# Softmax minus one-hot over 8192 rows: loads row by row, the sixth row in two column halves

## The chip, the cores and the metric

The kernel runs on one NeuronCore of a Trainium2 chip. The metric is the device time of one execution in microseconds (us). The runs before the change took 1247.62, 1247.97 and 1248.04 us, median 1247.97 us. A profiled execution beside them gives the trace that is read here; its span, from the first to the last recorded instruction of the core, is 1245.7 us.

The engines that matter are VectorE (DVE), ScalarE (ACT), SyncE (SP), which issues the loads, and the 16 DMA engines of the core, which carry out loads and stores alike. ScalarE issues the stores beside its computing. Each issuing engine has a DMA queue of its own: the profile calls SyncE's q1 and ScalarE's q10.

## The reference

The inputs are logits of 8 x 1024 x 8192 in float32 and one label for each of the 8192 positions. For each row of 8192 values the result is the softmax minus a one at the label:

```python
logits_max = np.max(logits, axis=-1, keepdims=True)
exp_logits = np.exp(logits - logits_max)
softmax = exp_logits / np.sum(exp_logits, axis=-1, keepdims=True)
...
one_hot[batch_idx, seq_idx, labels] = 1.0
return (softmax - one_hot).astype(np.float32)
```

So 268.44 MB are read, and as much is written.

## The kernel before

The 8192 positions are spread over 128 partitions. One "row" `t` of the kernel is a tile of 128 partitions x 8192 float32 values, 32 KB in each partition and 4 MB (4.19 million bytes) in all; there are T = 64 rows. Two rows (G = 2) make a batch `b`, and there are B = 32 batches. In DRAM the two rows of a batch lie behind one another for each partition, 64 KB in one run.

The tile `X` has three slots (SLOTS = 3) of two rows each, so six rows are in the chip at a time. Everything is done in place in `X`: a row is loaded, worked on and stored from the same place, and row `t` uses the place that row `t - 6` had.

For each row VectorE finds the negated maximum (TENSOR_REDUCE, writes `m`), ScalarE computes the exponential with its sum (ACTIVATE, `X<-X,m`), VectorE takes the reciprocal (writes `r`), ScalarE multiplies by it (ACTIVATE, `X<-X,r`), and VectorE subtracts the one-hot, made by comparing `iota` with the label (SCALAR_TENSOR_TENSOR). The loop of lines 160 to 190 writes the order of each engine out by hand: in step `t` VectorE has the reciprocal of `t`, the maximum of `t + 1`, the subtraction of `t`; ScalarE has the exponential of `t`, the issue of the store of `t - 1`, the scaling of `t`. Only the last row is scaled and subtracted in two halves.

Loads are issued on SyncE's queue, in order, by `load(b)` (lines 120 to 130). The letter of the string `LOADS` (line 13) tells how: `r` loads the two rows of a batch by one DMA each (32 KB a partition), `w` loads both by one DMA (64 KB a partition). Batches 0 to 4 and 26 to 31 are `r`, the 21 batches 5 to 25 are `w`. A load waits until the stores of what lay in its place are done: an `r` load for the store of one row, a `w` load for the stores of two. The sixth row's place (row 5) first holds the integers from which `iota` is made, so its load waits for the VectorE instruction that reads them (`w_iota`, line 98).

Stores go out on ScalarE's queue, one DMA for each row (`STORES` is all `r`, lines 132 to 143). The profile puts most instructions on line 68, in the helper `run`, so they are told apart by their tiles.

Of the kernel before, what the change touches and what calls it, by code (L numbers as in the profile page):

```python
# [7 lines left out]
P = 128  # L8
G = 2
SLOTS = 3  # L10


LOADS = "rrrrrwwwwwwwwwwwwwwwwwwwwwrrrrrr"
STORES = "rrrrrrrrrrrrrrrrrrrrrrrrrrrrrrrr"


@with_exitstack
def kernel(
    ctx: ExitStack,
    tc: tile.TileContext,  # L20
    logits: bass.AP,
    labels: bass.AP,
    out: bass.AP,
):
    nc = tc.nc
    fp32 = mybir.dt.float32
    i32 = mybir.dt.int32
    i16 = mybir.dt.int16
    Act = mybir.ActivationFunctionType
    Alu = mybir.AluOpType  # L30

    x_nv = logits.flatten_outer_dims()
    o_nv = out.flatten_outer_dims()
    N, V = x_nv.shape
    T = N // P
    B = T // G
    lab_bp = labels.rearrange("a b -> (a b)").rearrange("(b q) -> b q", q=G * P)
    x_b = x_nv.rearrange("(b p j) v -> b p j v", p=P, j=G)
    o_b = o_nv.rearrange("(b p j) v -> b p j v", p=P, j=G)

    const = ctx.enter_context(tc.tile_pool(name="const", bufs=1))
    psum = ctx.enter_context(tc.tile_pool(name="psum", bufs=1, space=bass.MemoryType.PSUM))


    X = const.tile([P, SLOTS, G, V], fp32)
    lab_raw = const.tile([B, G * P], labels.dtype)
    lab_f = const.tile([B, G, P], fp32)
    ident = const.tile([B, B], fp32)
    lab = const.tile([P, G, B], fp32)

    m, s, r = (const.tile([P, T], fp32, name=n) for n in ("m", "s", "r"))

    iota = psum.tile([P, V], i16)
    lab_ps = iota[:].bitcast(fp32)[:, :T].rearrange("p (j b) -> p j b", j=G)

    with tc.tile_critical():  # L56
        sem = tc.alloc_semaphore
        got = [[sem(f"got{i}{q}") for q in range(2)] for i in range(SLOTS)]
        put = [[sem(f"put{i}{q}") for q in range(2)] for i in range(SLOTS)]
        lab_got, dve, act, pe, pool = (sem(n) for n in ("lab_got", "dve", "act", "pe", "pool"))  # L60
        count = {}

        def run(engine, waits, counter, method, **operands):

            waits = list(dict.fromkeys(waits))
            for w in waits[:-1]:
                engine.wait_ge(*w)
            instruction = getattr(engine, method)(**operands)  # L68
            for w in waits[-1:]:
                instruction._wait_ge(*w)  # L70
            step = 16 if method == "dma_start" else 1
            instruction.then_inc(counter, step)
            count[counter.name] = count.get(counter.name, 0) + step
            return counter, count[counter.name]


        w_raw = run(nc.scalar, [], lab_got, "dma_start", out=lab_raw[:], in_=lab_bp)
        w = run(nc.gpsimd, [], pool, "memset", ap=ident[:], constant=0.0)
        w_ident = run(
            nc.gpsimd, [w], pool, "affine_select",  # L80
            out=ident[:], in_=ident[:], compare_op=Alu.not_equal, fill=1.0,
            base=0, pattern=[[-1, B]], channel_multiplier=1,
        )

        made = X[:, SLOTS - 1, G - 1, :].bitcast(i16)[:, :V]
        w_made = run(
            nc.gpsimd, [], pool, "iota", out=made, pattern=[[1, V]], base=0, channel_multiplier=0
        )
        step = mybir.dt.size(labels.dtype) // 4
        lab32 = lab_raw[:].bitcast(i32).rearrange("b (p j s) -> b j p s", j=G, s=step)  # L90
        w_lab = run(nc.vector, [w_raw], dve, "tensor_copy", out=lab_f[:], in_=lab32[:, :, :, 0])
        for j in range(G):
            w = run(
                nc.tensor, [w_ident, w_lab], pe, "transpose",
                out=lab_ps[:, j, :], in_=lab_f[:, j, :], identity=ident[:],
            )
        w_turned = run(nc.vector, [w], dve, "tensor_copy", out=lab[:], in_=lab_ps)
        w_iota = run(
            nc.vector, [w_turned, w_made], dve, "tensor_scalar",
            out=iota[:].bitcast(i32), in0=made.bitcast(i32), scalar1=0, scalar2=None, op0=Alu.bitwise_or,  # L100
        )


        every, rows = slice(0, P), slice(0, G)
        PIECES = {
            "r": [(every, slice(j, j + 1)) for j in range(G)],
            "h": [(slice(i, P, 2), rows) for i in range(2)],
            "w": [(every, rows)],
        }

        def meets(a, b):

            sets = [[set(range(*d.indices(n))) for d, n in zip(p, (P, G))] for p in (a, b)]
            return all(x & y for x, y in zip(*sets))


        loaded, stored, finished = {}, {}, []
        last_made = [((every, slice(G - 1, G)), w_iota)]

        def load(b):  # L120
            loaded[b] = []
            before = stored.get(b - SLOTS, last_made if b == SLOTS - 1 else [])
            for q, piece in enumerate(PIECES[LOADS[b]]):
                ps, js = piece
                free = [w for other, w in before if meets(piece, other)]
                w = run(
                    nc.sync, free, got[b % SLOTS][q], "dma_start",
                    out=X[ps, b % SLOTS, js, :], in_=x_b[b, ps, js, :],
                )
                loaded[b].append((piece, w))  # L130

        def store(t):
            b, j = divmod(t, G)
            stored.setdefault(b, [])
            for q, piece in enumerate(PIECES[STORES[b]]):
                ps, js = piece
                if js.stop != j + 1:
                    continue
                w = run(
                    nc.scalar, [finished[t]], put[b % SLOTS][q], "dma_start",  # L140
                    out=o_b[b, ps, js, :], in_=X[ps, b % SLOTS, js, :],
                )
                stored[b].append((piece, w))


        def row(t):
            return X[:, t // G % SLOTS, t % G, :]

        def row_max(t):
            b, j = divmod(t, G)  # L150
            arrived = [w for piece, w in loaded[b] if meets(piece, (every, slice(j, j + 1)))]
            return run(
                nc.vector, arrived, dve, "tensor_reduce",
                out=m[:, t : t + 1], in_=row(t), axis=mybir.AxisListType.X, op=Alu.max, negate=True,
            )


        load(0)
        w_max = row_max(0)
        for t in range(T):  # L160
            x = row(t)
            label = lab[:, t % G, t // G : t // G + 1]
            w = run(
                nc.scalar, [w_max], act, "activation",
                out=x, in_=x, func=Act.Exp, bias=m[:, t : t + 1], scale=1.0, accum_out=s[:, t : t + 1],
            )
            w_sum = run(nc.vector, [w], dve, "reciprocal", out=r[:, t : t + 1], in_=s[:, t : t + 1])
            if t + 1 < T:
                if (t + 1) % G == 0:
                    load((t + 1) // G)  # L170
                w_max = row_max(t + 1)
            if t > 0:
                store(t - 1)

            n = 1 if t + 1 < T else 2
            cols = [slice(i * V // n, (i + 1) * V // n) for i in range(n)]
            scaled = [
                run(
                    nc.scalar, [w_sum], act, "activation",
                    out=x[:, c], in_=x[:, c], func=Act.Copy, bias=0.0, scale=r[:, t : t + 1],  # L180
                )
                for c in cols
            ]
            for c, w in zip(cols, scaled):
                w = run(
                    nc.vector, [w], dve, "scalar_tensor_tensor",
                    out=x[:, c], in0=iota[:, c], scalar=label, in1=x[:, c],
                    op0=Alu.is_equal, op1=Alu.subtract, reverse1=True,
                )
            finished.append(w)  # L190
        store(T - 1)
        for b in range(B - SLOTS, B):
            for _, w in stored[b]:
                nc.scalar.wait_ge(*w)


# [28 lines left out]
```

## Time and profile before

| what | value |
|---|---|
| median of the runs | 1247.97 us (1247.62 to 1248.04) |
| span of the profiled execution | 1245.7 us |
| VectorE busy | 1119.2 us, 90% |
| ScalarE busy | 919.1 us, 74% |
| loads (q1) | 43 DMAs, 268.44 MB |
| stores and labels (q10) | 65 DMAs, 268.51 MB |
| mean DMA rate over the span | 431 GB/s |

"Busy" is the time in which an engine computes. A queue's share counts the time that its packets took, against 16 DMA engines over the whole span. In a table of windows the last two columns are the mean busy share of the 16 DMA engines and the bytes moved per time; a packet's bytes are counted when it ends, so short windows show shares a little over 1 and rates above or below the mean.

### The profile page before, as it was taken

How to read it: one execution, taken by the hardware profiler on the slowest of the kernel's cores; microseconds unless marked ns; L12 is line 12 of the kernel's file. 1: busy time of each engine (PE TensorE's matmuls, PEld its weight loads, DVE VectorE, ACT ScalarE, POOL GpSimd, SP SyncE). 2: the span in 40 equal slices, each digit the busy share in tenths (PEclk: the TensorE clock that was granted, in tenths of full speed). 3: DMA queues.
4: the chain of work that ended last, by engine and by line, in shares of the span. 5: the costliest groups of instructions: out<-in, count | busy, mean ns of one | idle time of the engine just before them, and what ended most of it. 6: DMA issues, size and time to landing. Idle time of an engine off the chain costs nothing.

```text
span 1245.7 us, 592 instructions
## 1 busy us (share of the span) xinstructions
PE 0.4 (0%) x2; PEld 0.3 (0%) x2; DVE 1119.2 (90%) x196; ACT 919.1 (74%) x194; POOL 7.4 (1%) x7
## 2 busy tenths in 40 slices
PE   0000000000000000000000000000000000000000
PEld 0000000000000000000000000000000000000000
DVE  5999998888988889888998888988889999999893
ACT  3888886778776787767877778777777788887772
POOL 2000000000000000000000000000000000000000
DMA  9999999999999999999999999999999999999998
GB/s 406 417 429 433 438 433 442 437 426 427 430 435 445 439 417 442 426 430 437 432 443 438 420 435 432 430 437 450 420 426 437 436 428 432 437 435 429 432 437 386
DMA packets 15460, 536.98 MB, mean 431 GB/s; under 512 B 1728, under 2 KB 1728, under 8 KB 1760
## 3 DMA queue, kind: packets, MB, share of 16 engines
q1 hardware_dynamic: 6192, 268.44, 50.0%
q10 hardware_dynamic: 9264, 268.51, 49.9%
q14 instruction: 4, 0.03, 0.0%
HBM read 268.50 MB, written 268.44 MB: 431 GB/s over the span
## 4 chain that ended last, share of the span: by engine, by line
DMA 59%; DVE 37%; another core or an unknown queue 2%; ACT 1%; DVEq 0%; issue 0%; PE 0%; SPq 0%; ACTq 0%
DMA X<-in_logits_dram 31%; DMA out_dram<-X 27%; DVE m L68 18%; DVE X L68 18%; ACT X L68 1%; DVE iota L68 0%; DVEq L56 0%; DMA lab_raw<-in_labels_dram 0%; DVE lab_f L68 0%; DVE r L68 0%; PE iota L68 0%; SPq L68 0%; ACTq L68 0%; DVE lab L68 0%
## 5 line engine op out<-in xcount | busy, mean ns | idle before, releaser
L68 DVE TENSOR_REDUCE m<-X 128x1 f32<-128x8192 f32 x64 | 555.2, 8675 | 94.3 <-DMA X<-in_logits_dram 94.3
L68 ACT ACTIVATE X<-X,m 128x8192 f32<-128x8192 f32 x64 | 455.9, 7123 | 188.4 <-DVE m L68 188.4
L68 DVE SCALAR_TENSOR_TENSOR X<-iota,lab,X 128x8192 f32<-128x8192 int16 (+1 forms) x65 | 559.7, 8612 | 4.1 <-ACT X L68 4.1
L68 ACT ACTIVATE X<-X,r 128x8192 f32<-128x8192 f32 (+1 forms) x65 | 456.0, 7017 | 115.9 <-DVE r L68 115.9
L68 DVE RECIPROCAL r<-s 128x1 f32<-128x1 f32 x64 | 9.9, 154 | 7.3 <-ACT X L68 7.3
L68 ACT ACTIVATION_READ_ACCUMULATOR X<-X,m 128x1 f32 x64 | 12.0, 187 | 0.0
L68 DVE CAST lab_f<-lab_raw 32x256 f32<-32x256 int32 x1 | 3.7, 3685 | 4.7 <-DMA lab_raw<-in_labels_dram 4.7
L68 POOL IOTA X<- 128x8192 int16 x1 | 6.9, 6944 | 0.0
L68 DVE TENSOR_SCALAR iota<-X 128x4096 int32<-128x4096 int32 x1 | 4.4, 4427 | 0.1
L68 ACT ACT_TABLE_LOAD x1 | 1.3, 1283 | 1.3 <-SPq L56 1.3
L68 DVE COPY lab<-iota 128x64 f32<-128x64 f32 x1 | 0.2, 225 | 0.5 <-PE iota L68 0.5
L68 PE MATMUL iota<-ident,lab_f 32*128 32x32 f32 x2 | 0.4, 300 | 8.5 <-DVE lab_f L68 8.5
L68 PEld LDWEIGHTS iota<-ident,lab_f 32*128 32x128 f32 x2 | 0.3, 196 | 8.4 <-DVE lab_f L68 8.4
L68 POOL TENSOR_SCALAR_AFFINE_SELECT ident<-ident 32x32 f32<-32x32 f32 x1 | 0.2, 204 | 0.1
L68 POOL MEMSET ident<- 32x32 f32 x1 | 0.1, 115 | 0.5 <-SPq L56 0.5
L209 POOL MEMSET const-bfloat16-1.0<- 128x1 bf16 x1 | 0.1, 107 | 0.0
L209 POOL MEMSET const-uint8-127<- 128x1 uint8 x1 | 0.1, 107 | 0.0
L209 POOL MEMSET const-float32-0.0<- 128x1 f32 x1 | 0.1, 104 | 0.2 <-issue 0.2
L209 POOL MEMSET const-float32-1.0<- 128x1 f32 x1 | 0.1, 104 | 0.0
## 6 DMA issues: line engine op xcount, KB each, us to landing
out_dram<-X ACTq DMA_DIRECT2D x64, 4096.0 KB, 30.8
X<-in_logits_dram SPq DMA_DIRECT2D x22, 4096.0 KB, 26.6
X<-in_logits_dram SPq DMA_DIRECT2D x21, 33.4
lab_raw<-in_labels_dram ACTq DMA_DIRECT2D x1, 64.0 KB, 3.8
```

Source lines behind the costliest of these rows:

```text
L68: instruction = getattr(engine, method)(**operands)
L209: nc = _bacc.Bacc("TRN2", target_bir_lowering=False, num_devices=1)
```

## The change

All loads become row loads, except that row 5, the second of batch 2, is loaded by two DMAs, one for the left 4096 columns and one for the right 4096 (16 KB a partition each). Both are issued on SyncE's queue, both wait for `w_iota`, and both count on the same semaphore, of which the maximum of row 5 waits for the full count. The 21 loads of two rows become 42 loads of one row, each waiting for the store of its own place alone. The number of load DMAs goes from 43 to 65. The computing, its order and the stores are the same; the helpers for pieces and their overlaps go away.

```diff
-LOADS = "rrrrrwwwwwwwwwwwwwwwwwwwwwrrrrrr"
-STORES = "rrrrrrrrrrrrrrrrrrrrrrrrrrrrrrrr"
+LOADS = "rr" + "c" + "r" * 29
...
+        full, left, right = slice(0, V), slice(0, V // 2), slice(V // 2, V)
         PIECES = {
-            "r": [(every, slice(j, j + 1)) for j in range(G)],
-            "h": [(slice(i, P, 2), rows) for i in range(2)],
-            "w": [(every, rows)],
+            "r": [(j, full) for j in range(G)],
+            "c": [(j, full) for j in range(G - 1)] + [(G - 1, left), (G - 1, right)],
         }
...
         def load(b):
-            loaded[b] = []
-            before = stored.get(b - SLOTS, last_made if b == SLOTS - 1 else [])
-            for q, piece in enumerate(PIECES[LOADS[b]]):
-                ps, js = piece
-                free = [w for other, w in before if meets(piece, other)]
-                w = run(
-                    nc.sync, free, got[b % SLOTS][q], "dma_start",
-                    out=X[ps, b % SLOTS, js, :], in_=x_b[b, ps, js, :],
+            i = b % SLOTS
+            for j, c in PIECES[LOADS[b]]:
+                t = b * G + j
+                free = [stored[t - SLOTS * G]] if b >= SLOTS else [w_iota] if t == SLOTS * G - 1 else []
+                loaded[t] = run(
+                    nc.sync, free, got[i][j], "dma_start",
+                    out=X[:, i, j, c], in_=x_b[b, :, j, c],
                 )
-                loaded[b].append((piece, w))
...
         def row_max(t):
-            b, j = divmod(t, G)
-            arrived = [w for piece, w in loaded[b] if meets(piece, (every, slice(j, j + 1)))]
             return run(
-                nc.vector, arrived, dve, "tensor_reduce",
+                nc.vector, [loaded[t]], dve, "tensor_reduce",
```

24 lines of the change are left out of this document (7 added, 17 removed).

## The prediction

> **What bounds the kernel now.** I read the page's busy times first, then its slices and queues.
>
> ```profile
> PE 0.4 (0%) x2; PEld 0.3 (0%) x2; DVE 1119.2 (90%) x196; ACT 919.1 (74%) x194; POOL 7.4 (1%) x7
> ...
> DMA  9999999999999999999999999999999999999998
> ...
> q1 hardware_dynamic: 6192, 268.44, 50.0%
> q10 hardware_dynamic: 9264, 268.51, 49.9%
> ```
>
> VectorE is busy for 90%, but the two DMA queues together fill 50.0 + 49.9 = 99.9% of the 16 DMA engines' time. Next come the windows, to see whether this holds where loads are rows and where they are pairs. The columns are the window, its length, the busy time of PE, PEld, DVE, ACT and POOL, then PE's clock, the DMA share and GB/s.
>
> ```profile
> 120.00:160.00 40.00, 0.00 (x0) 0.00 (x0) 40.00 (x8) 32.91 (x8) 0.00 (x0) 1.00 1.00 433
> 200.00:1000.00 800.00, 0.00 (x0) 0.00 (x0) 719.96 (x125) 594.92 (x125) 0.00 (x0) 1.00 1.00 433
> 1000.00:1220.00 220.00, 0.00 (x0) 0.00 (x0) 209.80 (x38) 174.70 (x39) 0.00 (x0) 1.00 1.00 433
> ```
>
> The first window lies among the early row loads, the second almost wholly among the pair loads, the third among the late row loads. The DMA share is 1.00 and the rate 433 GB/s in all three. From 120 to 160 VectorE even computed without a pause, and the rate was no other. So the bytes bound this kernel: 536.98 MB at 433 GB/s are 1240.1 us, and the span is 5.6 us more.
>
> VectorE's waits look like something that finer loads could win back:
>
> ```profile
> DVE m L68 <- DMA X<-in_logits_dram: 94.3, 25, 6.9
> SPq L68 <- DMA out_dram<-X: 699.1, 37, 57.3
> SPq L67 <- DMA out_dram<-X: 446.9, 21, 21.5
> ```
>
> The maximum waits 25 times for a load, 94.3 us in all; SyncE waits for stores nearly all the time (the 21 entries on line 67 are the first of the two waits of a pair load). But while they wait the DMA engines are at 1.00. An earlier issue only lengthens a queue that is already served without a gap.
>
> **The change part by part.**
>
> *Pair loads become row loads: packets.* Each of the 21 pair loads (128 packets of 64 KB) becomes two row loads (128 packets of 32 KB each). That adds 21 x 128 = 2688 packets, 168 on each DMA engine, and 21 completions. What these cost is bounded by two readings. The first is the pace of the chain of waits in the pair stretch:
>
> ```profile
> 159.71 0.02 issue
> 159.72 32.61 DMA X<-in_logits_dram
> ...
> 934.28 0.02 issue
> 934.29 32.60 DMA X<-in_logits_dram
> ```
>
> These are the issues of the first and the last pair load, 20 pairs apart: (934.29 - 159.72) / 20 = 38.73 us a pair, so 19.36 us a row. The late row loads are issued in the timeline of SyncE at
>
> ```profile
> 1115.11 0.33 SPq L68 DMA_DIRECT2D X<-in_logits_dram  x1
> ...
> 1173.13 0.33 SPq L68 DMA_DIRECT2D X<-in_logits_dram  x1
> ```
>
> with two issues between them: (1173.13 - 1115.11) / 3 = 19.34 us a row. By this reading the change saves 0.02 us on each of 42 rows, about 1 us. The second reading is the byte count in two windows of the DMA view, 200 to 960 (pairs) and 1000 to 1190 (rows):
>
> ```profile
> DMA packets 8449, 329.74 MB, mean 434 GB/s; under 512 B 928, under 2 KB 928, under 8 KB 928
> ...
> DMA packets 2820, 82.32 MB, mean 433 GB/s; under 512 B 307, under 2 KB 307, under 8 KB 307
> ```
>
> 329.74 MB / 760 us is 433.9 GB/s, 82.32 / 190 is 433.3: rows are 0.14% dearer. On the 42 rows, some 813 us, that is 1.1 us lost, less what the windows' edges make of it (one 32 KB packet on each engine is 0.5 MB, 0.6% of the smaller window, so the sign is not certain). Ends: -1 and +1 us. I take 0, as neither reading is closer to the edit than the other. The SyncE instructions beside it (22 more issues of 0.33 us) lie in time that SyncE spends waiting: 22 x 0.33 = 7 us against 1146 us.
>
> The Trainium skill ("DMA: Bandwidth & Descriptors", section "Rules for kernel authors", and the fit in "Anatomy of one DMA") speaks against the change: it asks for coalescing and gives each DMA about 2.0 us beside its bytes. By an estimate from that page, 22 more DMAs would add 44 us if nothing covered them, so 1292 us. The rows above do not agree for queued transfers: twice the number of load DMAs per byte ran at the same 433 GB/s.
>
> *Each row load waits for one store only.* In the pair stretch the first row's place lies free until the second is stored. After the change its load is issued about one row period, 19.3 us, earlier. The DMA engines have no empty time to put it into, so it is worth 0 in the middle; VectorE loses its long waits of up to 6.9 us and gets short ones at every row instead, like the late rows:
>
> ```profile
> 1180.42 8.69 DVE L68 TENSOR_REDUCE m<-X 128x1 f32<-128x8192 f32 x1 [1.92 <-DMA X<-in_logits_dram]
> ...
> 1199.76 8.69 DVE L68 TENSOR_REDUCE m<-X 128x1 f32<-128x8192 f32 x1 [1.93 <-DMA X<-in_logits_dram]
> ```
>
> If DMA were not the cover, the gain would be bounded by the 94.3 us of waits.
>
> *The sixth row in halves.* Its own packets, 8 more on each engine and one more completion, are a twentieth of the 168 above: under 0.1 us. What it does to the order is more. At 433 / 16 GB/s a 32 KB packet takes 1.21 us on an engine; a row has 8 for each engine, 9.69 us alone, and load plus store take 19.4 us, which is the period seen. So the two queues share an engine packet by packet where both are full. With 16 KB packets (0.61 us) the sixth load then gets a third of the engine and the stores two thirds. These rows give the place:
>
> ```profile
> 46.98 0.36 ACTq L68 DMA_DIRECT2D out_dram<-X  x1
> ...
> 64.29 0.34 ACTq L68 DMA_DIRECT2D out_dram<-X  x1
> ...
> 71.37 0.33 SPq L68 DMA_DIRECT2D X<-in_logits_dram  x1
> ...
> 81.60 0.34 ACTq L68 DMA_DIRECT2D out_dram<-X  x1
> ...
> 98.95 8.58 DVE m L68
> ```
>
> The first five loads keep the engines until about 2 + 5 x 9.69 = 50 us. Then the first store (issued at 46.98) and the sixth load share them. Before, the store was done at 71.37, when the seventh load goes out. Now 8 x (1.21 + 0.61) = 14.5 us serve it, and it is done some 5 us earlier; the second store, issued at 64.29, follows at once for another 14.5 us. In these 29 us the sixth load moves its 16 packets and ends near 80, not 71. Its reader, the maximum of row 5 at 98.95, has 18 us to spare. Later loads start 5 us late in the worst case; but the third store is issued only at 81.60, and until it begins the loads have the engines alone and win some of it back. I put the lasting delay of all loads at 2 to 4 us, and as much lead for the stores. No byte is lost by it. VectorE catches up with the loads some rows earlier, and again nothing waits that moves bytes.
>
> The skill's page "DMA: Bandwidth & Descriptors", section "Queues, rings and completion order", says that each engine goes round-robin between queues at packet granularity. The pace above agrees with an even share for equal packets (19.34 us against 19.4); whether it is per packet with half-size ones no row here shows, and with shares by bytes the delay would be 0.
>
> *The tail.* Here a delay can cost. The end is
>
> ```profile
> 1230.18 0.34 ACTq L68 DMA_DIRECT2D out_dram<-X  x1
> ...
> 1199.70:1230.20 30.50, 0.00 (x0) 0.00 (x0) 26.29 (x5) 20.13 (x5) 0.00 (x0) 1.00 1.01 435
> 1230.20:1246.00 15.80, 0.00 (x0) 0.00 (x0) 0.00 (x0) 0.00 (x0) 0.00 (x0) 1.00 0.76 330
> ```
>
> The last load lands at 1199.74, the last maximum starts at 1199.76, and its store goes out 30.4 us later. Meanwhile the DMA engines have older stores to do. After 1230.2 they move 330 x 15.8 = 5.21 MB, of which the last store is 4.19: 1.02 MB, 2.4 us, are left of older ones when it is issued. From the issue to the first packet I allow up to 1 us, since at the start
>
> ```profile
> 0.96 108.21 SPq L68 DMA_DIRECT2D X<-in_logits_dram  x9
> ...
> 1.00:2.00 1.00, 0.00 (x0) 0.00 (x0) 0.00 (x0) 0.65 (x1) 0.92 (x3) 1.00 0.05 14
> 2.00:3.00 1.00, 0.00 (x0) 0.00 (x0) 0.00 (x0) 0.63 (x1) 1.00 (x1) 1.00 1.85 575
> ```
>
> a load issued at 0.96 had whole packets done before 3. So the last load may land 1.4 us later before the engines run dry; each further us costs one. When does it land? With plain rows throughout, the issue of row 9's load at
>
> ```profile
> 128.24 0.33 SPq L68 DMA_DIRECT2D X<-in_logits_dram  x1
> ```
>
> plus 54 rows of 19.34 is 1172.6, against 1173.13 now. Early row loads land sooner after their issue (median of the first 200 us 24.2 us, late ones 26.6):
>
> ```profile
> X<-in_logits_dram SPq DMA_DIRECT2D x10, 4096.0 KB, 24.2
> ...
> X<-in_logits_dram SPq DMA_DIRECT2D x9, 4096.0 KB, 26.6
> ```
>
> So plain rows would land the last load about 2.5 us earlier, and the halves 2 to 4 later: -0.5 to +1.5. Less the 1.4 of slack that costs 0 to 0.1 us; with the worst delay of 5 it is 1.1. I take 0.2.
>
> **The sum** goes against the profiled execution: 1245.7 + 0 (packets) + 0.1 (halves) + 0.2 (tail) = 1246.0 us, range 1244.7 to 1247.9 (packets -1 to +1, halves 0.1, tail 0 to 1.1). The median of the runs is 1247.97 - 1245.7 = 2.27 us above the span, so 1248.3 us, 1247.0 to 1250.2.
>
> **Rivals.**
>
> *The tail runs dry (slower).* The halves delay all loads by more than I think, and nothing later takes it back, because each load follows a store and each store a load by the same fixed steps. From a late landing of 1.4 us on, each us counts. With the halves' full 29 us served before the seventh load and a worse order behind it, the last load would land 5 us later: 1248.0 + 5 - 1.4 = 1251.6 us. For it: the slack is small and the halves act on all later loads. Against: the stores gain the same lead, and plain rows start 2.5 us ahead. Chance 0.12.
>
> *Every DMA has a price that queueing does not hide (slower).* The least time of a load from issue to landing is 12.2 us (by the tile's view, first line below), 2.5 above 9.69; 22 x 2.5 = 55 us, 1303 us. Against: the equal pace of rows and pairs. Chance 0.01.
>
> ```profile
> DMA to landing us min/median/max: 12.2/32.6/60.1
> ```
>
> *The earlier issue pays (faster).* It would have to fill time in which engines idle: the 5.6 us beyond bytes / 433, of which start and end keep most. With 3 of them won, 1245 us. For it: the slow start between 40 and 80 us, below, which begins where the sixth row's load does, and which halves might smooth: 419 instead of 433 over 40 us is 1.3 us. Against: the share there is 1.00. Chance 0.05.
>
> ```profile
> 40.00:80.00 40.00, 0.00 (x0) 0.00 (x0) 40.00 (x7) 34.05 (x8) 0.00 (x0) 1.00 1.00 419
> ```
>
> **How the numbers follow.** A change of 0.2% is 2.5 us, about what a measurement can tell: 1245.5 to 1250.5 is "the same". The forecast, 1248.3 us, has 0.82, all of it within this bound; the two slower rivals have 0.13, the faster one 0.05. Most of what is left out of 1247.0 to 1250.2 lies on the slow side, and the share below reaches a little into it, so the range is 1246.8 to 1250.4.
>
> **What would show it.** Right: 65 loads, no window of 200 us between 60 and 1200 below 432 GB/s, a period of 19.3 us between issues on SyncE from 130 us on, waits of the maximum of 1 to 2.5 us at nearly every row, the seventh load's issue near 66 instead of 71.37, and a last store that begins while another still runs. Wrong: a gap in the DMA share behind about 1225 us (the tail), or a lower share or rate in the middle (a price for each DMA), or a rate above 434 there.

## The result, and the profile after

The changed kernel takes 1249.11 us in the median of 22 runs (1247.94 to 1258.57), the kernel before 1248.11 us beside it (22 runs, 1247.38 to 1248.97). The ratio is 1.0022 with an interval of 1.0013 to 1.0030: slower by 0.2%. The 22 times fall in two groups: 15 lie from 1247.94 to 1249.87, with a median of 1248.99, and 7 from 1253.05 to 1258.57. The median moved by 1.0 us; the mean, which the ratio follows, moved by 2.7 us (1250.8 against 1248.1), and most of that comes from the seven: the 15 alone have a mean of 1248.9. The profiled execution took 1249.06 us and is one of the first group. Its span is 1247.3 us, 1.76 us less than its time; by the same difference the profiled execution before, of span 1245.7 us, was one of 1247.5 us.

The page after the change shows the same picture in the large:

```profile
PE 0.4 (0%) x2; PEld 0.3 (0%) x2; DVE 1119.2 (90%) x196; ACT 919.0 (74%) x194; POOL 7.4 (1%) x7
...
q1 hardware_dynamic: 9360, 268.44, 50.0%
q10 hardware_dynamic: 9264, 268.51, 49.9%
```

VectorE and ScalarE are as busy as before, and the queues still fill 99.9% of the DMA engines. The windows (columns as before) say the same of the middle, but not of the end:

```profile
200.00:1000.00 800.00, 0.00 (x0) 0.00 (x0) 725.22 (x127) 596.24 (x127) 0.00 (x0) 1.00 1.00 433
...
1220.00:1232.00 12.00, 0.00 (x0) 0.00 (x0) 7.91 (x4) 7.77 (x4) 0.00 (x0) 1.00 1.01 434
1232.00:1236.00 4.00, 0.00 (x0) 0.00 (x0) 2.90 (x1) 0.00 (x0) 0.00 (x0) 1.00 0.70 303
```

Between 1232 and 1236 the DMA engines are idle for 30%, around the issue of the last store at 1234.94. (In these windows a packet's time and bytes count where the packet starts, not where it ends.) The kernel before has no such hole:

```profile
1232.00:1236.00 4.00, 0.00 (x0) 0.00 (x0) 0.00 (x0) 0.00 (x0) 0.00 (x0) 1.00 1.06 459
```

The timeline after the change gives the steps: the issues of the loads of rows 6, 7, 8 and 63, the last maximum and the last store.

```profile
67.17 0.33 SPq L67 DMA_DIRECT2D X<-in_logits_dram  x1
...
84.68 0.33 SPq L67 DMA_DIRECT2D X<-in_logits_dram  x1
...
105.44 0.33 SPq L67 DMA_DIRECT2D X<-in_logits_dram  x1
...
1170.72 0.33 SPq L67 DMA_DIRECT2D X<-in_logits_dram  x1
...
1204.53 8.69 DVE L67 TENSOR_REDUCE m<-X 128x1 f32<-128x8192 f32 x1 [1.94 <-DMA X<-in_logits_dram]
...
1234.94 0.34 ACTq L67 DMA_DIRECT2D out_dram<-X  x1
```

The seventh load goes out at 67.17 instead of 71.37: the first store is done 4.2 us earlier. At the end the last load is issued 2.4 us earlier than before (1170.72, 1173.13), yet its maximum starts 4.8 us later (1204.53, 1199.76). The loads stand longer in their queue, 33.8 us from issue to maximum instead of 26.6, while the stores are ahead. VectorE's waits for loads have not gone, they have been cut up:

```profile
DVE m L67 <- DMA X<-in_logits_dram: 96.5, 50, 2.3
```

96.5 us in 50 waits of at most 2.3, where it was 94.3 in 25 of at most 6.9.

The theory to test was thus (A): the halves of the sixth row lose turns to the stores, every later load is late by some us, and at the end the last row's chain, from its maximum to its store, is no longer covered by older stores. Its rival (B): the 42 row loads in place of 21 pair loads cost the time.

### The profile page after: what moved, and what is told of

It reads as the page before. It is cut to its first block, busy times and chain, and to the rows that moved or that the text cites. A ratio compares the mean times of both kernels' runs of the same rounds, so it can differ in the third digit from the quotient of the medians.

```text
span 1247.3 us, 593 instructions
## 1 busy us (share of the span) xinstructions
PE 0.4 (0%) x2; PEld 0.3 (0%) x2; DVE 1119.2 (90%) x196; ACT 919.0 (74%) x194; POOL 7.4 (1%) x7
## 4 chain that ended last, share of the span: by engine, by line
DMA 64%; DVE 34%; ACT 1%; DVEq 0%; issue 0%; PE 0%; ACTq 0%; SPq 0%
DMA out_dram<-X 37%; DMA X<-in_logits_dram 27%; DVE m L67 17%; DVE X L67 16%; ACT X L67 1%; DMA lab_raw<-in_labels_dram 1%; DVE iota L67 0%; DVEq L55 0%; DVE r L67 0%; DVE lab_f L67 0%; PE iota L67 0%; ACTq L67 0%; DVE lab L67 0%; ACTq L203 0%; DVEq L66 0%
## 5 line engine op out<-in xcount | busy, mean ns | idle before, releaser
L67 DVE TENSOR_REDUCE m<-X 128x1 f32<-128x8192 f32 x64 | 555.6, 8681 | 96.5 <-DMA X<-in_logits_dram 96.5
L67 DVE CAST lab_f<-lab_raw 32x256 f32<-32x256 int32 x1 | 1.1, 1143 | 7.3 <-DMA lab_raw<-in_labels_dram 7.3
```

## The experiments

### Plain rows

```diff
-LOADS = "rr" + "c" + "r" * 29
+LOADS = "r" * 32
```

> All 64 loads as plain rows, the sixth one whole. Theory A (the halves of row 5 delay every later load, the last maximum starts at 1204.5 instead of 1199.8 us, and the DMA engines idle before the last store): the last maximum starts at 1198 to 1200 us, the DMA engines have no gap before the last store, 1247.3 to 1248.3 us, and no execution above 1251. Theory B (42 row loads in place of 21 pair loads cost the time): 1249.1 us as after the change, also with executions at 1253 and above.

Measured: 1248.10 us in the median of 11 runs (1247.75 to 1248.50), ratio to the kernel before 0.9999 (0.9990 to 1.0008). Issues of loads 6, 9 and 63, the last maximum and the last store:

```profile
71.21 0.33 SPq L67 DMA_DIRECT2D X<-in_logits_dram  x1
...
128.09 0.33 SPq L67 DMA_DIRECT2D X<-in_logits_dram  x1
...
1174.92 0.33 SPq L67 DMA_DIRECT2D X<-in_logits_dram  x1
...
1199.14 8.69 DVE L67 TENSOR_REDUCE m<-X 128x1 f32<-128x8192 f32 x1 [1.94 <-DMA X<-in_logits_dram]
...
1229.56 0.34 ACTq L67 DMA_DIRECT2D out_dram<-X  x1
```

A holds and B falls: the row loads cost nothing that can be measured, and none of the 11 times is above 1249. Row 9's load goes out at 128.09, so the rows follow one another at (1174.92 - 128.09) / 54 = 19.39 us. Against this kernel the halves alone move the issue of the last load 4.2 us forward and the last maximum 5.4 us back.

### Halves in the kernel before

```diff
-LOADS = "rrrrrwwwwwwwwwwwwwwwwwwwwwrrrrrr"
+LOADS = "rrcrrwwwwwwwwwwwwwwwwwwwwwrrrrrr"
...
+            "c": [(every, slice(j, j + 1)) for j in (0, 1, 1)],
...
+                c = slice(0, V)
+                if LOADS[b] == "c" and q > 0:
+                    c = slice((q - 1) * V // 2, q * V // 2)
...
```

> The kernel before with the sixth row's load in halves and nothing else changed; the 21 pair loads stay. Theory A with a delay that lasts through any loads: last maximum at 1203 to 1205, 1249 to 1250 us. Theory A with the pair loads setting the order anew, since each waits for two stores: last maximum at 1199 to 1201, 1248.1 us, no execution above 1251. Theory B: 1248.1 us.

Measured: 1248.69 us in the median of 11 runs (1248.03 to 1250.06), ratio 1.0004 (0.9996 to 1.0013), and in the profiled execution

```profile
1200.66 8.69 DVE L68 TENSOR_REDUCE m<-X 128x1 f32<-128x8192 f32 x1 [1.96 <-DMA X<-in_logits_dram]
```

So the 21 pair loads set most of the order anew: the last maximum is 0.9 us later than before, not 5. The median's 0.6 us lies inside the interval and stays unassigned.

### The last row stored in halves

```diff
+                halves.append((c, w))
             finished.append(w)
-        store(T - 1)
+            halves = halves if t + 1 == T else []
+        b, j = divmod(T - 1, G)
+        for c, w in halves:
+            stored[T - 1] = run(
+                nc.scalar, [w], put[b % SLOTS][j], "dma_start",
+                out=o_b[b, :, j, c], in_=X[:, b % SLOTS, j, c],
+            )
```

> The changed kernel with the last row's store as two column halves, the first issued as soon as its half is subtracted, some 4.4 us ahead of the second. Theory A: the gap before the last store is filled, the end comes about 1.5 us earlier, 1247.5 us, and the slow executions lose up to 4 us each. Theory B: 1249.1 us, since the cost lies in the middle.

Measured: 1249.10 us in the median of 12 runs (1248.46 to 1254.37), ratio 1.0019 (1.0008 to 1.0031); 4 of the 12 at 1252.99 or above. This is a miss for A as I had put it. The issues and the windows of the tail:

```profile
1230.41 4.73 ACTq L67 DMA_DIRECT2D out_dram<-X  x2
...
1232.00:1236.00 4.00, 0.00 (x0) 0.00 (x0) 2.77 (x1) 0.00 (x0) 0.00 (x0) 1.00 0.92 393
1236.00:1240.00 4.00, 0.00 (x0) 0.00 (x0) 0.00 (x0) 0.00 (x0) 0.00 (x0) 1.00 0.99 422
```

Most of the hole is filled (0.92 instead of 0.70), and the time stays. So filling the hole does not win the loss of the first group back: the DMA engines themselves end later than with plain rows, hole or not. The stretch from 80 to 130, behind the halves, shows some of it. With plain rows, in the changed kernel, and here:

```profile
80.00:130.00 50.00, 0.00 (x0) 0.00 (x0) 50.00 (x10) 41.07 (x10) 0.00 (x0) 1.00 1.01 436
```

```profile
80.00:130.00 50.00, 0.00 (x0) 0.00 (x0) 50.00 (x10) 41.08 (x10) 0.00 (x0) 1.00 1.01 433
```

```profile
80.00:130.00 50.00, 0.00 (x0) 0.00 (x0) 50.00 (x10) 41.07 (x10) 0.00 (x0) 1.00 1.01 430
```

436 against 433 and 430 GB/s over 50 us are 0.3 and 0.7 us of the engines' mean. A store ends with the slowest of 16 engines, whose own loss these means don't show. The records of the single packets in the traces say something similar: added up over all packets of 16 KB and more, one of the 16 engines is busy for 1243.98 to 1244.51 us in the mean in the seven profiled executions of the changed kernel and for 1244.56 here, against 1243.82 with plain rows. So packets take 0.2 to 0.7 us longer in all. Why they do is not shown.

### Two rows halved

```diff
-LOADS = "rr" + "c" + "r" * 29
+LOADS = "rr" + "cc" + "r" * 28
```

> The changed kernel with row 7's load in halves too. Theory A: the loads are delayed by a second step of 4 to 6 us, the last maximum starts at 1208 to 1211, nothing is left to cover it, so 1253 to 1255 us. Theory B: 8 more packets on each engine, under 0.1 us, so 1249.1 us.

Measured: 1257.29 us in the median of 6 runs, but from 1253.96 to 1264.57; ratio 1.0081 (1.0060 to 1.0102). The profiled execution is the fastest, 1253.96 us:

```profile
1209.43 8.69 DVE L67 TENSOR_REDUCE m<-X 128x1 f32<-128x8192 f32 x1 [1.98 <-DMA X<-in_logits_dram]
...
1239.84 0.34 ACTq L67 DMA_DIRECT2D out_dram<-X  x1
```

The last maximum moves by a second step of 4.9 us, and the time by the same 4.9 against the changed kernel's 1249.06: nothing is left to cover it. A's number holds for this execution, the fastest; the median of 1257.29 lies above A's 1253 to 1255. The scatter was not expected. Two further executions show where it lies.

> Rows 5 and 7 halved, a second execution, for its place in the scatter from 1254 to 1265 us. If it is at 1256 or above: theory A expects a last maximum later than 1209.4 by as much as the time is above 1254; theory C expects the last maximum to move by less, and packets that take longer in some window of the middle or the start.

> Rows 5 and 7 halved, a third execution, with the same expectations: by theory A the last maximum moves as the time does, by theory C it moves by less and some window in the middle or at the start shows a lower rate.

They took 1256.88 and 1255.22 us, and their last maxima are

```profile
1212.34 8.69 DVE L67 TENSOR_REDUCE m<-X 128x1 f32<-128x8192 f32 x1 [1.95 <-DMA X<-in_logits_dram]
```

```profile
1210.69 8.69 DVE L67 TENSOR_REDUCE m<-X 128x1 f32<-128x8192 f32 x1 [1.94 <-DMA X<-in_logits_dram]
```

The times less the last maxima are 44.53, 44.54 and 44.53 us in the three executions. So in these three executions all of the scatter is a scatter in when the last load lands, as A says; for those up to 1264.57 there is no trace.

### Halves at row 41

```diff
-LOADS = "rr" + "c" + "r" * 29
+LOADS = "r" * 20 + "c" + "r" * 11
```

> Plain row loads, but the second row of batch 20 (row 41) in column halves in place of row 5. Theory A (half-size packets lose turns against full-size stores whenever both queues are full): all later loads are 5 to 9 us late, last maximum at 1204 to 1208, 1250 to 1254 us. If what costs is only the place at the start, beside the first stores, 1248.1 us as with plain rows.

Measured: 1253.43 us in the median of 4 runs (1253.28 to 1254.42), ratio 1.0046 (1.0031 to 1.0062). The time is as A has it; the last maximum, at 1208.89, is 0.9 us later than A's latest. In the waits and the timeline:

```profile
DVE m L67 <- DMA X<-in_logits_dram: 101.1, 47, 11.7
...
1208.89 8.69 DVE L67 TENSOR_REDUCE m<-X 128x1 f32<-128x8192 f32 x1 [1.92 <-DMA X<-in_logits_dram]
...
1239.30 0.34 ACTq L67 DMA_DIRECT2D out_dram<-X  x1
```

One wait of 11.7 us stands out, where plain rows have none above 2.6; it is of the size of one halved load's delay (29.1 - 19.4 = 9.7 us by the prediction's shares, plus the usual 1.9). It never comes back: the last maximum is 9.7 us later than with plain rows. Here both queues are full when the halves come, and the delay is the full 9.7; at row 5 it is 5.4. That it is less there because the store queue is empty for a while between the first stores is argued, not tested.

### The sixth row halved by partitions

```diff
-LOADS = "rr" + "c" + "r" * 29
+LOADS = "rr" + "p" + "r" * 29
...
-            "c": [(j, full) for j in range(G - 1)] + [(G - 1, left), (G - 1, right)],
...
+            "p": [(every, j) for j in range(G - 1)] + [(top, G - 1), (bottom, G - 1)],
...
-                    out=X[:, i, j, c], in_=x_b[b, :, j, c],
+                    out=X[ps, i, j, :], in_=x_b[b, ps, j, :],
```

Here `top` and `bottom` are partitions 0 to 63 and 64 to 127, with whole rows of 32 KB.

> The changed kernel with the sixth row's load as two DMAs of 64 partitions each, so that packets stay at 32 KB. Theory A (packet size against the stores' packets): no lasting delay, last maximum at 1198 to 1200, 1248.1 us, no execution above 1251. If two DMAs in place of one are what costs: 1249.1 us, with executions at 1253 and above.

Measured: 1255.21 us in the median of 5 runs (1254.81 to 1255.76), ratio 1.0059 (1.0047 to 1.0072). Neither expectation holds, since another effect lies on top. The window of the halved load, first here and then in the changed kernel:

```profile
48.00:82.00 34.00, 0.00 (x0) 0.00 (x0) 34.00 (x7) 28.08 (x7) 0.00 (x0) 1.00 1.00 325
```

```profile
48.00:82.00 34.00, 0.00 (x0) 0.00 (x0) 34.00 (x7) 28.08 (x7) 0.00 (x0) 1.00 1.00 417
```

While 64 partitions are loaded at a time, all traffic runs at 325 GB/s: (417 - 325) / 433 x 34 = 7.2 us of DMA time are lost, and the time is 7.1 us above that of plain rows. The packet records show where: from 52 to 80 us a 32 KB packet of a load takes 1.97 us in the mean, and one of a store 1.33, where both take 1.21 with plain rows. For the question, size of packets or number of DMAs, this run decides little. What speaks for A is the time less the last maximum, which starts at 1206.58: 48.61 us, near the 48.96 of plain rows and not the changed kernel's 44.53.

### The first store halved too

```diff
-            stored[t] = run(
-                nc.scalar, [finished[t]], put[i][j], "dma_start",
-                out=o_b[b, :, j, :], in_=X[:, i, j, :],
-            )
+            for c in (left, right) if t == 0 else (full,):
+                stored[t] = run(
+                    nc.scalar, [finished[t]], put[i][j], "dma_start",
+                    out=o_b[b, :, j, c], in_=X[:, i, j, c],
+                )
```

> The changed kernel with the first row's store in column halves as well, so that the halves of the sixth load meet packets of their own size (16 KB) in the store queue. Theory A: the queues share evenly again, the seventh load goes out near 71 us instead of 67, the last maximum starts at 1198 to 1201 us, 1248.1 us, no execution above 1251. If halved packets or the additional DMA cost by themselves: 1249.1 us or more, with executions at 1253 and above.

Measured: 1248.35 us in the median of 11 runs (1248.20 to 1248.56), ratio 1.0006 (0.9997 to 1.0015).

```profile
71.74 0.33 SPq L67 DMA_DIRECT2D X<-in_logits_dram  x1
...
1199.24 8.69 DVE L67 TENSOR_REDUCE m<-X 128x1 f32<-128x8192 f32 x1 [1.94 <-DMA X<-in_logits_dram]
```

The halves of the sixth row are still there, and so is the additional DMA. Only the store that they meet has packets of their own size, and the delay is gone: seventh load at 71.74, last maximum at 1199.24, no time above 1249. So it is the unequal size of the packets in the two queues that shifts the order. The queue rows of the DMA view from 53 to 65 us show the sharing itself, in the changed kernel and then here (packets, MB, share of the 16 engines):

```profile
q10 hardware_dynamic: 112, 3.67, 70.8%
q1 hardware_dynamic: 112, 1.57, 30.6%
```

```profile
q10 hardware_dynamic: 179, 2.67, 51.9%
q1 hardware_dynamic: 184, 2.51, 48.8%
```

In both the two queues move about as many packets as each other. But in the changed kernel the load gets 1.57 MB through and the store 3.67, a third against two thirds; with packets of one size it is 2.51 and 2.67 MB. (Some of the packets have four bytes and close a DMA: 16 of the load's 112.)

For the time the run says less. The kernel before took 1247.50 us beside it (median of 15 runs), so 1248.35 is 0.85 us above that, inside the interval. Three executions of the changed kernel beside it took 1248.71 to 1249.20, all above its highest. So equal packets take away the late loads, all executions at 1253 and above, and some 0.6 us of the 1.4 between these medians; whether halved packets or more DMAs cost the other 0.85 by themselves is not settled. A second execution,

> The changed kernel with the first store in halves too, a second execution beside the others of this call: 1248.2 to 1248.6 us and a last maximum at 1199.2, as before; packets of 16 KB alone bring no scatter by theory A, and by theory C some.

took 1248.35 us with its last maximum at 1200.20, 1.0 us later than expected. The kernel before took 1247.35 us beside it, in a single run.

### Further executions of the changed kernel

> The changed kernel once more, for the profile of another execution: its times fall in two groups, about 1249 (15 of 22) and 1253 to 1258 us (7 of 22). If this one is of the second group, theory A (late loads, an idle stretch before the last stores) expects the last maximum 5 us or more later than 1204.5 and DMA idle time of 5 us or more after 1220; theory C (DMA engines slowed somewhere in the middle) expects a rate below 432 GB/s in some window of 200 us and no gap at the end.

> As the first repeat of the changed kernel: a look for an execution of the group at 1253 to 1258 us, with the same expectations.

> A further look at the changed kernel for an execution of the group at 1253 to 1258 us. Theory A there: last maximum at 1209 or later and idle DMA time near the end. Theory C: a lower rate in some window in the middle and no gap at the end.

> A further look at the changed kernel, with the same expectations: by theory A a late last maximum and a gap near the end, by theory C a lower rate in the middle and no gap.

> A further look at the changed kernel, again with the same expectations: by theory A a late last maximum and a gap near the end, by theory C a lower rate in the middle and no gap.

> The changed kernel, a further execution: about 1249 us with a last maximum at 1204, or 1253 to 1258, where theory A expects a last maximum at 1209 or later and theory C the same 1204 and a lower rate earlier.

They took 1249.14, 1249.16, 1248.71, 1248.92, 1249.20 and 1248.57 us: all six are of the first group, so the second has no profile. Still they show what sets the end. In a table with the others (time of the profiled execution, start of the last maximum, difference; the kernel before with its 1247.5 worked out above):

| kernel | time | last maximum | difference |
|---|---|---|---|
| before | 1247.5 | 1199.76 | 47.7 |
| plain rows | 1248.10 | 1199.14 | 48.96 |
| first store halved too | 1248.20 | 1199.24 | 48.96 |
| the same, second execution | 1248.35 | 1200.20 | 48.15 |
| halves in the kernel before | 1248.24 | 1200.66 | 47.58 |
| sixth row halved by partitions | 1255.19 | 1206.58 | 48.61 |
| changed, profile above | 1249.06 | 1204.53 | 44.53 |
| changed, six more | 1248.57 to 1249.20 | 1203.87 to 1204.63 | 44.53 to 44.84 |
| last row stored in halves | 1249.32 | 1204.39 | 44.93 |
| halves at row 41 | 1253.41 | 1208.89 | 44.52 |
| two rows halved | 1253.96 to 1256.88 | 1209.43 to 1212.34 | 44.53 to 44.54 |

The bare chain from the last maximum to the end is 44.53 us, and no kernel with a whole last store is below 44.52. Where the difference is larger, the DMA engines set the end. So the time is the later of two ends: what the DMA engines need without a gap, and the last maximum plus 44.53. With plain rows the first is 1248.1 us, so the two would meet at a last maximum of 1203.6, and there are 4.4 us to spare. In the changed kernel the two ends nearly coincide: five of its seven executions end with the bare chain, to 0.01 us, and two have 44.75 and 44.84, so there the DMA engines end last, at 1249.20 and 1248.71; with the last row in halves it is 1249.32.

## Why the prediction was right or wrong

*What bounds the kernel* was right: the DMA rate from 200 to 1000 us is 433 GB/s in every variant, and none came out measurably faster than before.

*Packets* at 0, between -1 and +1 us: right. Plain rows measure 0.9999. The 2 us for each DMA, of "DMA: Bandwidth & Descriptors" in the Trainium skill, don't appear for queued transfers: 21 more DMAs cost nothing that can be measured. The page gives this figure as a fit for DMAs that GpSimd issues, and asks for coalescing of many small transfers; here SyncE issues loads of 4 MB, so neither is stated for this case.

*One store to wait for* at 0: right. The waits became short and many, as forecast, and their sum stayed.

*The halves* shifted the order by the mechanism that the prediction describes. Row 6's load went out at 67.17, where "some 5 us earlier" than 71.37 and near 66 had been forecast. The period of 19.4 us, from which the prediction read the sharing by packet, does not show it: any division between the queues gives the same sum. The skill's section "Queues, rings and completion order" of the same page states turns between queues at packet granularity. The trace agrees, with the profile's packet of one 16 or 32 KB run: as many packets from each queue, with 1.57 MB against 3.67, and between the runs with unequal and with equal packets 5.4 us of delay against 0.1. (The page's packet is a group of descriptors, typically 9 to 17; in the records here the turn passes after each single run.) The sixth load's last packet ends at 80.7 us, as forecast. The lasting delay of the loads was put at 2 to 4 us; it is 5.4, a little beyond the prediction's worst case of 5.

*The tail* is the step that failed, in both of its numbers. First the landing: plain rows were said to land the last load 2.5 us earlier than before. They start the last maximum only 0.6 us earlier (1199.14, 1199.76). With 5.4 for the halves the sum is +4.8, where -0.5 to +1.5 was forecast. Of the two terms behind the 2.5 us, the 24.2 us from issue to landing are right (1199.14 - 1174.92); the time of the issue is not. It was put at 1172.6, by a pace of 19.34 us read from three late rows; the pace is 19.39, and over 54 rows this makes the 2.3 us by which the issue, at 1174.92, is later. Second the slack: 1.4 us was forecast, from 1.02 MB left after the last issue less 1 us for its start. A window counts a packet where it starts, so what the engines had begun before 1230.2 was left out; by the packet records 1.42 MB of older stores, 3.3 us, were still to do. (For the same reason the load issued at 0.96 had no whole packet done before 3: its first one starts at 2.15.) The rows show the slack more directly. From the issue of the last store to the end of the span it takes 1245.7 - 1230.18 = 15.5 us before and 1247.3 - 1234.94 = 12.4 us after the change; with halves at row 41 it is 1251.6 - 1239.30 = 12.3. A store alone needs the 12.4, so 3.2 us were slack. The late landing of 4.8 less 3.2 is 1.6 us, where the forecast had 0.2. That this is the difference of the two spans follows from how it is worked out. It says when the last store ends, not that the tail alone costs this: with the last row in halves the hole was nearly filled and the time stayed.

*No byte is lost*, and *under 0.1 us* for the halves' own packets, is the other term that was too small, as far as the records go. The packets of the changed kernel take 0.2 to 0.7 us longer in all than those of plain rows, and with the chain off the end the time is still about 0.8 us above theirs. And the prediction had no term for a scatter: 7 of the 22 times lie 3 us and more above the others and make most of the 2.7 us in the mean. With plain rows, and with equal packets, no time does, in 11 runs each.

*The zero point* was off too. The 2.27 us from span to median of runs took the profiled execution for a median one; with 1.76 it was a run of 1247.5, 0.5 us below the median. The two errors partly cancel, so the forecast of 1248.3 stands only 0.8 us from the measured median.

*The rivals.* "The tail runs dry" is what happened, with the gap behind 1225 us that the prediction named as a sign, and with 1249.1 in place of 1251.6, since its last load 5 us late was right and its slack too small. The other rivals, a price for every DMA and a gain from earlier issue, fell with the plain rows.

*What stays open.* First, the last row in halves took the chain off the end and still ran at 1248.9 us in the median of its 8 runs below 1251. So with the halves the DMA engines end some 0.8 us later than with plain rows even without the hole. Of the 1.0 us of the median, then, either end would give nearly all, and how much belongs to the late chain is not shown. The lower rate from 80 to 130 us and the longer packets are argued to be a part of it, and with equal packets 0.85 us above the kernel before remain. Second, the seven runs at 1253 to 1258: a last load that lands 4 to 9 us later would give them by the 44.53, and with two rows halved such a scatter is shown. Their tie to the unequal packets is shown by the two kernels without them, which have none in 22 runs; the path is not. If it were the late last load, the last row in halves should have won part of it back, and its four runs of this group are at 1253.0 to 1254.4 as well. None of them was profiled.

## What to carry to other kernels

Where two DMA queues keep the engines full, the sizes of their packets set their shares, and a single transfer with halved packets moves the order of all that follows by several us for good, when each row's load waits for one row's store; with loads of two rows, which wait for two stores, only 0.9 us of it were left. The late loads set the end only when the last one lands so late that the chain behind it is longer than the stores that cover it. So read the slack first: the time from the last store's issue to the end, against what a store alone takes.

## What the runs showed of the hardware that was not expected

A load of 64 partitions, 0 to 63 and then 64 to 127, lowered all traffic of the 16 engines from 417 to 325 GB/s while it lasted, although its packets were 32 KB like the others: they took 1.97 us each in place of 1.21. And a first delay of a few us did not heal over 1100 us in which the DMA engines were never idle: with row 41 halved a wait of 11.7 us became a last maximum 9.7 us late, to the end.
